# Splitting the attention logits, and a second feed-forward stage with six of its blocks by seven products

## The chip, the cores and the metric

The kernel runs on one core of one Trainium2 chip. The metric is the time of one execution on the device in microseconds (us). TensorE (PE in the profile) multiplies matrices; PEld is its loading of the stationary operand. VectorE (DVE), ScalarE (ACT) and GpSimd (POOL) do elementwise work. SyncE (SP) starts most of the transfers; GpSimd starts those that add into their target. Each engine works through a list of its own in order and waits on semaphores for the others.

## The reference, cut to what matters

One layer of a diffusion backbone: a half-step feed-forward layer, a mixer (attention beside an mLSTM), a second half-step feed-forward layer, a final norm. There are 256 latent tokens (x) and 256 context tokens (ctx), the width is 2048, the hidden width of a feed-forward layer 5632. All is in float32.

```python
def half_step_ffn(x, mod, i, g, w_up, w_down):
    h = adaln(x, g, mod, i)
    a, b = jnp.split(h @ w_up, 2, axis=-1)
    return x + 0.5 * mod[:, i + 2, None, :] * ((jax.nn.silu(a) * b) @ w_down)

def attend(q, k, v):
    s = jnp.einsum('bqhgd,bkhd->bhgqk', q, k, preferred_element_type=jnp.float32) * HEAD_DIM ** -0.5
    p = jax.nn.softmax(s, axis=-1).astype(v.dtype)
    return jnp.einsum('bhgqk,bkhd->bqhgd', p, v)
```

The second feed-forward layer and the attention have latent queries only (256 of them). There are 8 heads of 128, keys and values for 2 groups of 4 heads, and 512 keys. The modulation vectors mod[0] to mod[8] are products of a condition vector with nine 2048 by 2048 matrices; mod[8] is the gate of the second feed-forward layer's output.

## The kernel before, in words

**Split products.** A float32 product at full precision is made of three products of operands in the faster type fp32r: every operand x is split into hi (x rounded, by ACT) and lo (x minus hi, by DVE), and `mm3` (line 145) issues hi by hi, hi by lo and lo by hi. Weights are split as they arrive: `load_split` (line 138) has SP fetch 1 MB (128 by 2048) into one of 3 `raw` tiles, and `split` (line 117) turns it, in two halves of 1024 columns, into `hi` and `lo` tiles. There are four tiles of each, so four halves: ACT can start on a half when TensorE has released the half four before it. All rows of this splitting have the line numbers 125 (ACT) and 126 (DVE), all rows of the three products 147, 148 and 149.

**The order of the work.** The functions are Python generators that issue instructions unit by unit. A planner then orders each engine's list by program order and by when it reckons that operands are ready; an instruction marked `keep_in_program_order` stays where the program put it. Tiles of a pool with the same tag share a fixed number of slots, and a new tile waits for the slot's last reader.

**The attention.** `ev_kv` (line 1591) and `ev_q` (line 1603) norm and rotate keys and queries, turn them by TensorE transposes, and a DVE copy puts the turned tile into `kT` or `qT` in plain float32. `attention` (line 1648) then makes the logits of one head and 128 queries by 512 keys with one plain float32 product (line 1655), the softmax, its transposes and the product with the values `av`. There are 16 such logits. `kT` and `av` lie in the slot that the context half of `v1` (the mLSTM's values) has left; `qT` in the slot of `mqT`. While the queries are made, half of `hhi` and `hlo` (the normed input, 512 tokens) holds context columns that nobody reads any more.

**The second feed-forward stage.** The hidden width is cut into 11 blocks of 512 numbered 0 to 10. Block 0 is done ahead. Each other block's up projection is made in one of two ways:

- `up(n)` (line 2126): eight units, each of 1 MB of weights and 24 matmuls of 512 columns.
- `quad(n)` (line 2046): a Winograd form of the 2 by 2 product (tokens halves by width halves) that needs seven products instead of eight. Fourteen steps, each of 1 MB of weights and 12 matmuls. The sums of weights that it needs are made by transfers which add into the tile that they land in (`accum`, line 723, from GpSimd's queue): `chain_[q]` holds weights, is split, gets the next part added, is split again. The order of steps and what follows each is the table `order` at line 2103; X and Y are two banks of PSUM, each with one buffer, that the steps accumulate into and that ACT and DVE read out between steps.

`down(n)` (line 2160) is the down projection of a block: four units of 1 MB and 24 matmuls. It needs the block's hidden values in transposed form, which `turned` (line 2015) makes by transposes and a split into the two-slot tiles `hids`; a list `turn` keeps what waits for that. The loop at line 2204 issues unit after unit of `units` (ups and downs) and behind each the quad steps that are due by `PACE2` (line 39): step number below (u + 1) times 70/73. Quads are 1, 3, 5, 7, 9; ups are 2, 4, 6, 8, 10.

Beside this, `mod_late` (line 264) sums the 32 products of mod[8], one DVE instruction each, paced by calls of `load_split`; the pair (32, 62) says that product 32 is due at call 62, and two waits of 3 calls come on top. After the loop `before_final` (line 2191) drains what is left of them, writes the row of mod[8] to DRAM and has it spread from there over all partitions into `g8`, in the slot of `chain_[0]`. The down projection of block 9 and then that of block 10 (`last2`, line 2219) follow; they read `g8`, and in block 9 each finished piece gets the residual added by a transfer.

Of the kernel before, what the change touches and what calls it, by code (L numbers as in the profile page):

```python
# [19 lines left out]
P = 128  # L20
# [18 lines left out]
PACE2 = 70 / 73  # L39
# [17 lines left out]
def tile_layer(ctx: ExitStack, tc: tile.TileContext, I: dict, out: bass.AP):  # L57
# [1189 lines left out]
    with ExitStack() as mx:  # L1247
# [11 lines left out]
        v1 = {s: one([P, 2, NH, 130], f"v1{s}", tag="v1l" if s else "slotA") for s in (CTX, LAT)}  # L1259
        for s in (CTX, LAT):  # L1260
            nc.gpsimd.memset(v1[s][:, :, :, 128:130], 1.0)

        def ev_mv(h0, c0, bs):
            for t, b in bs.items():
                if c0:
                    nc.vector.tensor_tensor(gt[:, t, :], b[:, :32], gb, op=ALU.add)
                s, tt = divmod(t, 2)
                nh = (b.shape[1] - c0) // HD
                nc.scalar.activation(v1[s][:, tt, h0 : h0 + nh, 0:HD], b[:, c0:].rearrange("p (h d) -> p h d", d=HD), AF.Copy)
# [134 lines left out]
        def state(h, kTc):  # L1404
# [7 lines left out]
            for t in range(2):  # L1412
                for d in range(2):
                    nc.vector.tensor_scalar(vw[:, t, d, :], v1[CTX][:, t, h, :], wg[:, t, d, h : h + 1], None, op0=ALU.mult)
# [93 lines left out]
        def heads_out(h, t, E, A):  # L1508
            b = tbank()
            for d in range(2):  # L1510
                o = b[:, d * 130 : (d + 1) * 130]
                srcs = [(q, st_) for q, (st_, t_) in enumerate(PAIRS[d]) if t_ == t]
                for n, (q, st_) in enumerate(srcs):
                    nc.tensor.matmul(o, E[:, d, q, :], v1[LAT][:, st_, h, :], start=d == 0 and n == 0, stop=False, skip_group_check=True)
# [76 lines left out]
        def ev_kv(t, b):  # L1591
# [3 lines left out]
            def late():  # L1595
# [3 lines left out]
                nc.vector.tensor_copy(kT[:, :, t * P : (t + 1) * P], tb[:, :256].rearrange("p (g k) -> p g k", g=2))  # L1599
# [3 lines left out]
        def ev_q(c, t, b):  # L1603
            y = head_norm(b, 4, 0, t - 2)

            def late():
# [3 lines left out]
                nc.vector.tensor_copy(qT[:, 4 * c : 4 * c + 4, (t - 2) * P : (t - 1) * P], tb.rearrange("p (g k) -> p g k", g=4))  # L1610
# [8 lines left out]
        kvs = one([P, NKV * 512 + 4 * 256], "kvs", tag="slotA")  # L1619
        kT = kvs[:, : NKV * 512].rearrange("p (g k) -> p g k", g=NKV)  # L1620
        av = kvs[:, NKV * 512 :].rearrange("p (t c) -> p t c", t=4)
# [20 lines left out]
        qT = one([P, NH, T], "qT", tag="mqT")  # L1642
# [5 lines left out]
        def attention(kv):  # L1648
            items = [(t, g) for t in range(2) for g in range(4)]
            pr, pT, o = {}, {}, {}  # L1650
            for i in range(len(items) + 2):
                if i < len(items):
                    t, g = items[i]
                    b = bank()
                    nc.tensor.matmul(b, qT[:, 4 * kv + g, t * P : (t + 1) * P], kT[:, kv, :], start=True, stop=True)
# [243 lines left out]
    with f2x:  # L1899
# [53 lines left out]
        beside["load"] = mod_late(f8cm.__enter__(), 8, 9, ((32, 62),))  # L1953
# [3 lines left out]
        QUADS = range(1, LAST, 2)  # L1957
# [54 lines left out]
        turn = []  # L2012
        summed = set()

        def turned():
# [3 lines left out]
            n, t, sa, sign = turn[0]  # L2019
            if n >= 2 and n - 2 not in summed or n - 1 not in hids or (n - 1, 0) in [x[:2] for x in turn] or (n - 1, 1) in [x[:2] for x in turn]:  # L2020
                return
# [17 lines left out]
        def wait_turn(n, t, sa, sign):  # L2039
            turn.append((n, t, sa, sign))  # L2040
# [5 lines left out]
        def quad(n):  # L2046
# [40 lines left out]

            def again(q):
                if n + 2 in QUADS:
                    nc.sync.dma_start(chain_[q], part(n + 2, 0, q))  # L2090
# [6 lines left out]
            def plain(q):  # L2097
# [8 lines left out]
                (n1, held, "Y", True, chained(1, 2), kept),  # L2106
                (s4, loaded, "Y", False, lambda q: accum(ra[q], part(n, 1, q)), p35),
# [106 lines left out]
        while turn:  # L2214
            turned()
# [156 lines left out]
```

## Time and profile before

| what | value |
|---|---|
| median of 3 runs | 2615.98 us (2615.42 to 2619.67) |
| the profiled execution's own time | 2617.32 us |
| its span, first to last instruction | 2615.6 us |
| granted TensorE clock, mean | 0.996 |
| the attention's queries and logits | about 1700 to 1850 us |
| the second feed-forward stage | about 1940 us to the end |

The profile lists for each engine the busy time, for groups of instructions the count, mean duration and the idle time before them, and who ended that. Matmuls are pipelined: a row's duration (0.39 us for 512 columns) overlaps the next one's, so their price is read from the distance between starts. Rows of a timeline are: start, duration, engine, line, operation, result and operands, count.

### The profile page before, as it was taken

The page shows a single profiled execution, that of the slowest core. Times are in us where ns is not written, and L with a number is a line of the kernel's source. Part 1 is how long each engine was busy: PE and PEld are TensorE (multiplying, and loading weights), DVE is VectorE, ACT ScalarE, POOL GpSimd, SP SyncE. Part 2 cuts the span into 40 slices and gives each one's busy share as a digit, 9 for nine tenths or more (in the row PEclk, how much of TensorE's full clock was granted, in tenths as well). Part 3 has the DMA queues.
Part 4 walks back from the last instruction along what each step waited for, and adds up shares of the span by engine and source line. Part 5 has one row for each costly group of instructions (what it writes and reads, how often), then busy time and mean ns, then how long its engine had stood idle before and what let it go on. Part 6 is the DMA issues. An engine that isn't in the chain of part 4 may idle for free.

```text
span 2615.6 us, 33733 instructions
## 1 busy us (share of the span) xinstructions
PE 2593.2 (99%) x12727; PEld 2155.0 (82%) x12727; DVE 2117.8 (81%) x2856; ACT 1361.1 (52%) x1724; POOL 209.1 (8%) x263
## 2 busy tenths in 40 slices
PE   8999999999999999999999999999999999999998
PEld 5788888888888888888889889887898888888887
DVE  7788888878888788888887789788888777777867
ACT  5454444445444465444454437555576655555554
POOL 0000000100000100000110000120000000000001
PEclk8999999999999999999999999999999999999999
DMA  9989999999999998889986856665679998989975
GB/s 396 350 213 267 269 278 279 258 271 284 269 275 281 266 246 237 229 210 230 227 242 265 297 198 240 207 214 203 237 251 301 312 291 278 286 286 281 271 229 175
DMA packets 127219, 679.97 MB, mean 260 GB/s; under 512 B 14152, under 2 KB 16712, under 8 KB 65232
## 3 DMA queue, kind: packets, MB, share of 16 engines
q1 hardware_dynamic: 99696, 500.59, 51.6%
q0 software_dynamic: 27360, 177.22, 34.6%
q8 instruction: 100, 1.64, 0.2%
q14 instruction: 63, 0.52, 0.1%
HBM read 659.87 MB, written 17.89 MB: 259 GB/s over the span
## 4 chain that ended last, share of the span: by engine, by line
PE 88%; DVE 5%; DMA 4%; issue 2%; ACT 1%; POOL 0%; SPq 0%; POOLq 0%; ACTq 0%; DVEq 0%
PE mm L149 23%; PE mm L147 23%; PE mm L148 23%; DMA mraw<-in_w_m 2%; DVE lo L126 1%; PE mm L85 1%; PE tr L148 1%; PE Y L149 1%; PE Y L147 1%; PE Y L148 1%; PE tr L149 1%; PE tr L147 1%; PE X L147 1%; PE X L149 1%; PE X L148 1%
## 5 line engine op out<-in xcount | busy, mean ns | idle before, releaser
L125 ACT ACTIVATE hi<-raw 128x1024 fp32r<-128x1024 f32 (+3 forms) x536 | 556.6, 1042 | 601.4 <-PE mm L149 440.4
L126 DVE TENSOR_TENSOR lo<-raw,hi 128x1024 fp32r<-128x1024 f32 (+1 forms) x524 | 631.4, 1210 | 273.4 <-ACT hi L125 248.5
L125 ACT ACTIVATE hi<-chain 128x1024 fp32r<-128x1024 f32 x320 | 338.1, 1060 | 259.9 <-PE mm L149 141.1
L126 DVE TENSOR_TENSOR lo<-chain,hi 128x1024 fp32r<-128x1024 f32 x320 | 386.2, 1220 | 84.9 <-ACT hi L125 82.3
L147 PE MATMUL mm<-hi,hhi 128*128 128x512 f32 (+3 forms) x1024 | 394.1, 385 | 0.0
L149 PE MATMUL mm<-hi,hlo 128*128 128x512 f32 (+3 forms) x1024 | 387.0, 378 | 0.0
L148 PE MATMUL mm<-lo,hhi 128*128 128x512 f32 (+3 forms) x1024 | 386.8, 378 | 0.0
L205 DVE SCALAR_TENSOR_TENSOR junk<-sraw,cBh 128x1024 fp8e5<-128x1024 f32 x192 | 234.2, 1220 | 22.2 <-DMA sraw<-in_w_mt 19.9
L149 PEld LDWEIGHTS mm<-hi,hlo 128*128 128x128 f32 x1024 | 192.5, 188 | 33.8
L147 PEld LDWEIGHTS mm<-hi,hhi 128*128 128x128 f32 x1024 | 192.6, 188 | 31.2 <-issue 0.2
L148 PEld LDWEIGHTS mm<-lo,hhi 128*128 128x128 f32 x1024 | 192.8, 188 | 30.9 <-issue 0.2
L149 PE MATMUL mm<-hi,hid2l 128*128 128x512 f32 x352 | 137.4, 390 | 0.0
L147 PE MATMUL mm<-hi,hid2h 128*128 128x512 f32 x352 | 137.2, 390 | 0.0
L148 PE MATMUL mm<-lo,hid2h 128*128 128x512 f32 x352 | 137.1, 390 | 0.0
L148 PE MATMUL mm<-lo,h2hi 128*128 128x512 f32 x320 | 124.8, 390 | 0.6 <-DVE lo L126 0.6
L147 PE MATMUL mm<-hi,h2hi 128*128 128x512 f32 x320 | 124.8, 390 | 0.0
L149 PE MATMUL mm<-hi,h2lo 128*128 128x512 f32 x320 | 124.6, 390 | 0.0
L723 POOL DMA_DIRECT2D chain<-in_w_up1b x60 | 53.1, 885 | 723.3 <-DVE lo L126 645.5
L147 PE MATMUL mm<-hhi,hi 128*128 128x512 f32 (+1 forms) x288 | 101.1, 351 | 0.0
L149 PE MATMUL mm<-hhi,lo 128*128 128x512 f32 (+1 forms) x288 | 99.0, 344 | 0.0
L148 PE MATMUL mm<-hlo,hi 128*128 128x512 f32 (+1 forms) x288 | 98.8, 343 | 0.0
L205 DVE SCALAR_TENSOR_TENSOR sr<-sr,cBl 128x1024 f32<-128x1024 f32 x65 | 78.2, 1216 | 7.9 <-DMA gains<-in_k_gain 6.4
(499 smaller groups left out, 5458.6 us busy)
## 6 DMA issues: line engine op xcount, KB each, us to landing
raw<-in_w_dn SPq DMA_DIRECT2D x70, 1024.0 KB, 7.5
sraw<-in_w_mt SPq DMA_DIRECT2D x128, 512.0 KB, 7.9
chain<-in_w_up1b POOLq DMA_DIRECT2D x60, 1024.0 KB, 10.5
raw<-in_w_up2b SPq DMA_DIRECT2D x50, 1024.0 KB, 6.7
raw<-in_w_up1b SPq DMA_DIRECT2D x40, 1024.0 KB, 8.1
mraw<-in_w_m SPq DMA_DIRECT2D x32, 1024.0 KB, 7.6
sr<-in_w_mt SPq DMA_DIRECT2D x62, 512.0 KB, 5.5
chain<-in_w_dn POOLq DMA_DIRECT2D x30, 1024.0 KB, 9.9
```

The source lines that it names most:

```text
L85: ins = getattr(self.engine, name)(*a, **k)
L125: scalar[0].activation(hi, src, AF.Copy)
L126: vector[0].tensor_tensor(lo, src, hi.bitcast(F32), op=ALU.subtract)
L147: tensor[0].matmul(out_ap, sh, mh, start=first, stop=False, skip_group_check=skip)
L148: tensor[0].matmul(out_ap, sh, ml, start=False, stop=False, skip_group_check=skip)
L149: tensor[0].matmul(out_ap, sl, mh, start=False, stop=last, skip_group_check=skip)
L205: ins = nc.vector.scalar_tensor_tensor(junk() if junk else raw, raw, 1.0, cB[s], op0=ALU.mult, op1=ALU.mult, accum_out=mT[:, i, s, kt, h : ...
L723: accum = lambda dst, src: nc.gpsimd.dma_start(dst, src, accum_op=ALU.add)
```

## The change

Four things in one edit:

- **Logits.** The turned keys and queries are split into hi and lo (`high_low`: one ACT copy and one DVE subtraction) and the logits are made by `mm3`, three products in fp32r, in place of one in float32. The split keys and the first four heads' queries lie in the context columns of `hhi` and `hlo`; the other queries take the slot of `mqT`; the second group's keys are copied by ACT into `k1` before `hhi` is given back. `v1`'s context half becomes two tiles, whose slots `av` and `k1` take.
- **Blocks.** Quads are 1, 3, 5, 6, 8, 9; ups are 2, 4, 7, 10. So one block goes from `up` to `quad`. The order of units becomes up 2, down 0, up 4, down 1 to 3, up 7, down 4 to 6, up 10, down 7 and 8.
- **Pace.** Steps start six units later and are due by (u - 6) times 84/62 with units counted from 1: 84 steps in 62 units in place of 70 in 73. A step that needs a hidden tile turned waits for it (`ready`), and a hidden tile is turned one unit (after a quad) or two (after an up) later than it could be. The products of mod[8] are due later: product 1 at call 14, product 32 still at call 62.
- **A sum of weights.** In each quad, the transfer that added a part into `chain_[q]` after the step n1 goes. The same sum is made from the part that lies in `ra[q]` anyhow: for q = 0 by two GpSimd additions of 128 by 1024, for q = 1 by one DVE addition of 128 by 2048.

```diff
-PACE2 = 70 / 73
+PACE2 = 84 / 62
...
-                nc.vector.tensor_copy(kT[:, :, t * P : (t + 1) * P], tb[:, :256].rearrange("p (g k) -> p g k", g=2))
+                w = (slice(4 + t // 2, 8, 2), slice(t % 2 * P, (t % 2 + 1) * P))
+                high_low(hhi[:, *w], hlo[:, *w], tb[:, :256].rearrange("p (g k) -> p g k", g=2))
...
-                nc.vector.tensor_copy(qT[:, 4 * c : 4 * c + 4, (t - 2) * P : (t - 1) * P], tb.rearrange("p (g k) -> p g k", g=4))
+                w = slice((t - 2) * P, (t - 1) * P)
+                qh, ql = queries(c)
+                high_low(qh[:, :, w], ql[:, :, w], tb.rearrange("p (g k) -> p g k", g=4))
...
+        def high_low(hh, hl, x):
+            nc.scalar.activation(hh, x, AF.Copy)
+            nc.vector.tensor_tensor(hl, x, hh.bitcast(F32), op=ALU.subtract)
...
+        k1 = one([P, 2, 2, T], "k1", F32R, tag="slot1")
+        for x in range(2):
+            nc.scalar.activation(k1[:, x], keys[1][x].bitcast(F32), AF.Copy)
+        keys[1] = [k1[:, x] for x in range(2)]
...
-                    nc.tensor.matmul(b, qT[:, 4 * kv + g, t * P : (t + 1) * P], kT[:, kv, :], start=True, stop=True)
+                    qs = [x[:, g, t * P : (t + 1) * P] for x in queries(kv)]
+                    mm3(b.rearrange("p (a k) -> p a k", a=2), *qs, *keys[kv], True, True)
...
-        beside["load"] = mod_late(f8cm.__enter__(), 8, 9, ((32, 62),))
+        beside["load"] = mod_late(f8cm.__enter__(), 8, 9, ((1, 14), (32, 62)))
...
-        QUADS = range(1, LAST, 2)
+        QUADS = (1, 3, 5, 6, 8, 9)
...
-            turn.append((n, t, sa, sign))
+            turn.append((n, t, sa, sign, at_unit[0] + 1 + (sign > 0)))
...
+            def summed_weights(q):
+
+                if q:
+                    tc.keep_in_program_order(add(chain_[q], chain_[q], ra[q]))
+                else:
+                    for h in range(2):
+                        w = slice(h * 1024, (h + 1) * 1024)
+                        nc.gpsimd.tensor_tensor(chain_[q][:, w], chain_[q][:, w], ra[q][:, w], op=ALU.add)
+                accum(ra[q], part(n, 1, q))
...
-                (n1, held, "Y", True, chained(1, 2), kept),
-                (s4, loaded, "Y", False, lambda q: accum(ra[q], part(n, 1, q)), p35),
+                (n1, held, "Y", True, None, kept),
+                (s4, loaded, "Y", False, summed_weights, p35),
...
-            yield from up(2)
-            yield from down(0)
-            for n in (4, 6, 8):
+            for n, downs in ((2, (0,)), (4, (1, 2, 3)), (7, (4, 5, 6)), (10, (7, 8))):
                 yield from up(n)
-                yield from down(n - 3)
-                yield from down(n - 2)
-            yield from down(7)
-            yield from up(10)
-            yield from down(8)
+                for d in downs:
+                    yield from down(d)
...
+        def ready(i):
+
+            n, step = i // 14, i % 14
+            if step == 11:
+                return (QUADS[n], 0) in done
+            return not n or step not in (1, 7) or (QUADS[n - 1], step // 7) in done
...
-        for u, _ in enumerate(units()):
+        for u, _ in enumerate(units(), 1):
             steps(forms)
+            at_unit[0] = u
             turned()
-            while n_side < n_quads and n_side < (u + 1) * PACE2:
+            while n_side < n_quads and n_side < (u - 6) * PACE2 and ready(n_side):
                 next(side)
                 n_side += 1
                 turned()
```

More of the change, by code (lines that the diff above doesn't have):

```diff
@@ L1258, in tile_layer @@
         gt = one([P, 4, 32], "gt")
[L1259 removed]
+        v1l = one([P, 2, NH, 130], "v1l")
+        v1 = {CTX: [one([P, NH, 130], f"v1c{t}", tag=f"slot{t}") for t in range(2)], LAT: [v1l[:, t] for t in range(2)]}
         for s in (CTX, LAT):
[L1261 removed]
+            for t in range(2):
+                nc.gpsimd.memset(v1[s][t][:, :, 128:130], 1.0)
         def ev_mv(h0, c0, bs):
```

30 lines of the change are left out of this document (19 added, 11 removed).

## The prediction, made before the changed kernel ran

> **What bounds the kernel now.** I read the page first (shares, chain of waits), then what TensorE waited for, then windows over stages, then single instructions.
>
> ```profile
> span 2615.6 us, 33733 instructions
> PE 2593.2 (99%) x12727; PEld 2155.0 (82%) x12727; DVE 2117.8 (81%) x2856; ACT 1361.1 (52%) x1724; POOL 209.1 (8%) x263
> PE 88%; DVE 5%; DMA 4%; issue 2%; ACT 1%; POOL 0%; SPq 0%; POOLq 0%; ACTq 0%; DVEq 0%
> ...
> PE mm L148 <- DVE lo L126: 0.6, 1, 0.6
> ...
> ACT hi L125 <- PE mm L149: 183.7, 128, 3.0
> ...
> 100.00:1000.00 900.00, 898.08 (x4113) 738.57 (x4112) 745.07 (x922) 452.68 (x526) 77.78 (x88) 1.00 0.95 267
> 600.00:650.00 50.00, 50.00 (x230) 41.33 (x229) 45.09 (x62) 25.03 (x29) 2.64 (x3) 1.00 0.97 296
> 1940.00:2616.00 676.00, 665.65 (x3002) 550.75 (x3001) 521.25 (x566) 373.74 (x403) 43.03 (x50) 1.00 0.88 270
> 2050.00:2500.00 450.00, 450.00 (x2011) 372.11 (x2010) 344.28 (x368) 251.65 (x259) 27.02 (x31) 1.00 0.93 282
> ```
>
> TensorE is busy 99% and the chain is 88% TensorE. The line of PE's waits is the only one from 1950 us to the end: 0.6 us. The ACT line (same stage) says that the splitting of weights stands still because TensorE has not released its buffers: ACT and DVE run ahead and are held back, not the reverse. In the windows (columns: PE, PEld, DVE, ACT, POOL busy; clock; DMA share; GB/s) the second feed-forward stage has TensorE at 450.00 of 450 with DVE at 76.5% and the transfers at 93%. The first stage, built in the same way, has TensorE at 898.08 of 900 with DVE at 83%, and one 50 us stretch with DVE at 90% and no loss. So a matmul saved is time saved, and what is laid on DVE is free up to some 90%, as long as it doesn't come in lumps that eat the lead.
>
> **The change part by part.**
>
> ```profile
> 1953.08 0.39 PE L147 MATMUL X<-hi,h2hi 128*128 128x512 f32 x1
> ...
> 1955.80 0.39 PE L147 MATMUL mm<-hi,h2hi 128*128 128x512 f32 x1
> ...
> 1961.23 0.39 PE L147 MATMUL X<-hi,h2hi 128*128 128x512 f32 x1
> ...
> 1739.48 1.02 PE L1655 MATMUL mm<-kvs,qT 128*128 128x512 f32 x2
> 1740.34 0.60 PE L1669 MATMUL tr<-ident,pr 128*128 128x128 f32 x4
> ```
>
> *One block from up to quad.* From the first to the second row is one quad step, 12 matmuls: 2.72 us; to the third one up unit, 24 matmuls: 5.43 us. So 0.2265 us a matmul. An up is 8 units, 192 matmuls, 43.5 us; a quad 14 steps, 168 matmuls, 38.1 us. Saved: **5.4 us**. Both are followed by the same eight transposes. The stage goes from 76 units and 70 steps to 68 and 84.
>
> *Logits.* A float32 logit (two records) takes 1740.34 - 1739.48 = 0.86 us up to the next start; three fp32r matmuls of 512 columns take 3 x 0.2265 = 0.68 us. 16 x 0.18 = **2.9 us** saved. Bounds: 0 if the moving operand in two pieces of 256 costs its overhead again, 3.0 at most; I take 2.9, as plain matmuls of that size are the nearest row.
>
> ```profile
> L1610 DVE COPY qT<-tr 128x512 f32<-128x512 f32 x4 | 2.8, 692 | 0.6 <-PE tr L1609 0.5
> L1770 ACT ACTIVATE cathi<-cx 128x512 fp32r<-128x512 f32 x4 | 2.4, 624 | 0.3 <-DVE cx L1714 0.2
> 1700.00:1850.00 150.00, 150.00 (x758) 121.26 (x757) 122.34 (x209) 79.91 (x117) 18.61 (x20) 1.00 0.61 213
> ```
>
> *What feeds the logits.* The DVE copy (0.69 us for 512 columns) becomes an ACT copy (0.62 by the nearest row) and a DVE subtraction of about the old length: four of 512 and four of 256 columns, and two copies of 512 into `k1`. That is about 4 x 0.62 + 4 x 0.35 + 2 x 0.62 = 5 us more on ACT, in 150 us in which it works 80. Cost 0, covered by TensorE's projections; what can be late is the first logit of a group, by one 0.6 us operation, and it has other matmuls to change places with. Without that cover it would be two groups x 0.7 = 1.4 us.
>
> ```profile
> 2572.02 2.28 DVE L2231 TENSOR_TENSOR lo<-raw,hi 128x2048 fp32r<-128x2048 f32 x1
> ...
> q1 hardware_dynamic: 22076, 137.91, 54.0%
> q0 software_dynamic: 6912, 44.04, 33.6%
> chain<-in_w_up2b POOLq DMA_DIRECT2D x30, 1024.0 KB, 10.9
> chain<-in_w_up2b SPq DMA_DIRECT2D x10, 1024.0 KB, 6.3
> ra<-in_w_up2b POOLq DMA_DIRECT2D x10, 1024.0 KB, 11.4
> ```
>
> *Load of the other engines.* From 1 MB of weights DVE subtracts 2.28 us' worth. In the dense part (61 units, 84 steps: 61 x 5.43 + 84 x 2.72 = 560 us) there are 145 MB against 136 in 560 us before: +20 us; the DVE additions +6 x 2.28 = 14; the read-outs of more quads about +4. With 76.5% before that makes about 83%, the first stage's level. Transfers: adding ones go from 8 x 5 = 40 (the x30 and x10 from GpSimd's queue) to 6 x 6 = 36, plain ones of weights from 106 to 104. With MB and the share of 676 us in the q rows, at 0.336 x 676 / 44 = 5.2 us a MB for the adding and 0.54 x 676 / 138 = 2.6 for the plain that is 26 us of transfer time less in a stage 8 us shorter: 88% becomes 85%. No price. The next quad's first weights now have two steps to land (13 us, 17 before) against 6.3; four steps separate an adding transfer from its use (27 us) against 10.9 to 11.4. Both still fit.
>
> *Steps later and closer.* The products of mod[8] are packed into some 54 calls in place of 60, 0.1 us of DVE a unit. Steps run beside units 7 to 68, with their transfers on SP's and GpSimd's queues behind those units' loads. The first six units lose DVE work, so the 0.6 us wait goes (worth up to 0.6, not counted). Two steps now often follow each other without a unit between them. By the order table that matters where the second writes a bank that is still read out: a12 to n1 and n1 to s4, four places in all by the pace. Bounds 0 to 1.3 us each (one 0.7 us read-out and its wait); taken 0, because the next unit's matmuls are ready and in another bank.
>
> *The sum by GpSimd.* This is the only new wait.
>
> ```profile
> L1617 POOL TENSOR_TENSOR gm<-gm,mg x4: 1293/1516/1745, 1726.9 to 1757.5; 128x512 f32<-128x512 f32 x4
> ...
> 1728.80 2.31 DVE L126 TENSOR_TENSOR lo<-raw,hi 128x1024 fp32r<-128x1024 f32 x1
> ...
> 1756.05 3.18 POOL L1617 TENSOR_TENSOR gm<-gm,mg 128x512 f32<-128x512 f32 x2 [26.01 <-ACT gm L1616]
> ...
> 1757.99 2.32 DVE L126 TENSOR_TENSOR lo<-raw,hi 128x1024 fp32r<-128x1024 f32 x1
> ...
> L125 ACT ACTIVATE hi<-chain 128x1024 fp32r<-128x1024 f32 x320 | 338.1, 1060 | 259.9 <-PE mm L149 141.1
> L126 DVE TENSOR_TENSOR lo<-chain,hi 128x1024 fp32r<-128x1024 f32 x320 | 386.2, 1220 | 84.9 <-ACT hi L125 82.3
> ```
>
> GpSimd's one elementwise product of this kind takes 1.29 to 1.75 us for 512 columns, so an addition of 1024 about 2.6 to 3.5, two a quad 5 to 7 us. It starts when n1's split has read `chain_[0]`, four steps before s2 reads the sum, so the sum itself is never late, and the adding transfer queued behind it on GpSimd has four steps. But DVE: while GpSimd ran to 1759.23, a split issued at 1757.99 took 2.32 us in place of 1.22: it stood still until GpSimd ended (1759.23 + 1.1 = 1760.3). So per quad DVE may stand still for up to 5 us, in two lumps, and has the 2.28 us addition later. The lead that can hide it: three halves of 1.36 (step) or 2.72 us (unit), 4.1 to 8.2, less ACT's 1.06 and DVE's 1.22 for a split: 1.8 to 5.9 us. Bounds: 0 a quad, and 7.3 - 1.8 = 5.5 a quad (33 us). Nearest row: this one and its twin at 1728.80, where a held split cost TensorE nothing. I take 0.2 a quad, **1 us**. The Trainium skill ("SBUF — State Buffer", Who interferes with whom) says the same as the row, that a VectorE instruction with two SBUF inputs and a GpSimd one that reads SBUF lock each other out whole; the two rows agree with it. The Trainium skill ("GPSIMD Engine Reference", 3.1 Elementwise) has 4497 ns for an addition of 2048 columns on GpSimd, by which the two would be an estimated 4.5 us a quad, a little under the 5 to 7 of the rows.
>
> *The end.*
>
> ```profile
> 2497.64 1.22 DVE L205 SCALAR_TENSOR_TENSOR sraw<-sraw,cBl 128x1024 f32<-128x1024 f32 x1
> ...
> g<-mod SPq DMA_DIRECT2D x1, 1024.0 KB, 4.8
> mod<-gr SPq DMA_DIRECT2D x1, 8.0 KB, 3.1
> L1022 DVE SCALAR_TENSOR_TENSOR acc<-acc,g x8: 679/682/692, 2566.4 to 2587.0; 128x512 f32<-128x512 f32 x8
> ...
> 2540.48 0.68 DVE L2048 TENSOR_TENSOR ca<-Y,ca 128x512 f32<-128x512 f32 x1
> ...
> 2544.30 0.69 DVE L2032 SCALAR_TENSOR_TENSOR hid2l<-tr,hid2h 128x512 fp32r<-128x512 f32 x1 [0.81 <-ACT hid2h L2030]
> ```
>
> Before, the last step came four units ahead of the final downs; now it is the very last thing before them. Its read-out up to the split hidden tile takes 4.5 us (2540.48 to 2544.99), and only the token half t = 0 of block 9 can cover it: two pieces of 2.72 us, enough if the planner puts them there; 0 to 4.5. The last product of mod[8] falls on call 68, now the last unit: product, sums, transpose (about 3 us), store 3.1, load 4.8 make 11 us, and the first use is some 11 us later; late by 0 to 4, with four PSUM banks (10.9 us) behind it. Taken 0.
>
> Sum: -5.4 - 2.9 + 1 = -7.3. The profiled execution (span 2615.6, itself 2617.32) would come to 2610.0; it lies 1.3 above the median. From the median 2615.98: **2608.6 us**.
>
> **The rivals.**
>
> *GpSimd holds DVE back (slower).* Place: between n1 and s4 of each quad. For it: the 2.32 us row, and DVE at 83% plus 6 x 5 to 7 us of standing still, which is 89 to 91%. Against it: 90% was carried without loss in the first stage. It decides from (8.3 + 5.2) / 6 = 2.3 us of TensorE a quad, where the 8.3 saved are gone and 5.2 (0.2%) more; at 2.3 to 5.5 a quad the time is 2621 to 2641. Between 0.5 and 2.3 a quad it gives 2611 to 2621, no change that can be told. The rule of the Trainium skill on "SBUF — State Buffer" is this mechanism in general form.
>
> *The end is laid bare.* Read-out chain and `g8` together 4 to 8 us: 2613 to 2617, no change.
>
> *The logits do not get cheaper.* 2.9 us less gain: 2611.5. Nothing speaks for it but the two-piece operand.
>
> **How the numbers follow.** Forecast (all but 3 us of the 8.3 kept) 0.60; end bare 0.12; GpSimd middling 0.10, heavy 0.16; logits 0.02. About 0.2% (5.2 us) is what measurement can tell here: faster 0.60, same 0.24, slower 0.16. The range goes from 2605 (8.3, the 0.6 us wait, a little luck) to 2620, leaving the heavy case and a few hundredths out.
>
> **What would show it.** Right: 24 fewer up or quad matmuls and no L1655 float32 rows; steps still 2.72 us apart; PE's waits in the stage under 2 us; DVE about 83%. Wrong: lo rows of 2.3 us and more beside the GpSimd additions with PE waits on DVE lo; a gap in PE just ahead of block 9's down, ended by DVE or by the load of `g8`; PE waits on the read-outs of X or Y.

## The result and the profile after

The changed kernel takes 2625.62 us (median of 6, 2621.68 to 2630.77) against 2616.03 for the kernel before (median of 6, 2615.42 to 2619.67): the ratio is 1.0038, with an interval from 1.0028 to 1.0047. It is slower by 9.6 us where 7.3 us of gain were forecast. The profiled execution took 2623.24 us, 2.4 under its median.

From the page of the changed kernel, the span, the shares and the chain of waits, and the group of the second stage's lo by hi matmuls:

```profile
span 2621.5 us, 33785 instructions
PE 2590.5 (99%) x12719; PEld 2152.0 (82%) x12719; DVE 2164.4 (83%) x2878; ACT 1378.6 (53%) x1750; POOL 238.6 (9%) x273
...
PE 84%; DVE 7%; DMA 5%; issue 2%; ACT 1%; POOL 0%; ACTq 0%; POOLq 0%; DVEq 0%
...
L148 PE MATMUL mm<-lo,hid2h 128*128 128x512 f32 x352 | 138.3, 393 | 8.0 <-DVE lo L126 7.8
```

TensorE has less to do (12719 matmul records against 12727, 2590.5 us busy against 2593.2), and the span is longer all the same: the chain went from 88% TensorE to 84%, DVE's share from 5 to 7%. The chain only points the way: one per cent of the span is 26 us, and its shares move by more than the loss from one kernel to another (94% TensorE on the page of the kernel with the logits alone).

The timelines' rows of the second stage's first and last matmul of 512 columns, first of the kernel before, then of the changed one:

```profile
1947.61 0.40 PE L147 MATMUL mm<-hi,h2hi 128*128 128x512 f32 x1
...
2605.86 0.39 PE L149 MATMUL mm<-hi,hid2l 128*128 128x512 f32 x1
```

```profile
1943.66 0.40 PE L147 MATMUL mm<-hi,h2hi 128*128 128x512 f32 x1
...
2611.66 0.39 PE L149 MATMUL mm<-hi,hid2l 128*128 128x512 f32 x1
```

The stage took 668.0 us in place of 658.3. With a block as a quad it should have taken 658.3 - 5.4 = 652.8, so 15.2 us are lost in it. (What lies ahead of the stage varies by up to 7.6 us from one profiled execution to the next, so in what follows the stage is measured from its own first to its own last matmul, and whole kernels are compared by their medians.)

What TensorE waited for from 1930 us to the end, in the changed kernel (total, times, longest), and one window of it:

```profile
PE mm L148 <- DVE lo L126: 8.3, 9, 2.4
PE Y L148 <- DVE lo L126: 0.7, 1, 0.7
PE tr L2052 <- DVE ca L2074: 0.5, 1, 0.5
PE Y L147 <- ACT cy L2087: 0.4, 2, 0.2
PE mm L147 <- ACT hid2h L2055: 0.2, 1, 0.2
...
2000.00:2500.00 500.00, 491.15 (x2181) 401.99 (x2180) 410.98 (x407) 291.95 (x309) 58.87 (x42) 1.00 0.85 267
```

Before, there was one such wait of 0.6 us. Now TensorE waits nine times for a `lo` in mm. DVE is busy 82% of the window (410.98 of 500), close to the 83% that were forecast, but not for the reasons forecast: a split that stands still counts as busy, and 12 splits of the stage, all beside GpSimd's additions, took 19.7 us more in sum than the usual 1.22 us each. Without standing still DVE would be at some 78%, while the forecast had 83% without it and 89 to 91% with it. The transfers are at 85% in this window, but the same window of the kernel with the logits alone has 93%; over the whole stage (1940 us to the end) they are at 82%, where 85% was forecast and 88% stood before. So the engines had less to do than was reckoned, and the stage lost all the same.

One of the places, in the timeline of the changed kernel (TensorE, DVE, GpSimd):

```profile
2004.74 0.73 PE L147 MATMUL mm<-hi,hid2h 128*128 128x512 f32 x2
2007.92 0.51 PE L148 MATMUL mm<-lo,hid2h 128*128 128x512 f32 x1 [2.44 <-DVE lo L126]
...
2003.78 2.95 DVE L126 TENSOR_TENSOR lo<-chain,hi 128x1024 fp32r<-128x1024 f32 x1 [0.62 <-ACT hi L125]
2006.65 1.21 DVE L126 TENSOR_TENSOR lo<-raw,hi 128x1024 fp32r<-128x1024 f32 x1
2007.79 0.68 DVE L2073 TENSOR_TENSOR ca<-Y,ca 128x512 f32<-128x512 f32 x1
2008.39 2.82 DVE L126 TENSOR_TENSOR lo<-raw,hi 128x1024 fp32r<-128x1024 f32 x1
...
2003.24 2.40 POOL L2120 TENSOR_TENSOR chain<-chain,ra 128x1024 f32<-128x1024 f32 x1 [16.45 <-DVE lo L126]
2006.81 3.31 POOL L2120 TENSOR_TENSOR chain<-chain,ra 128x1024 f32<-128x1024 f32 x1 [1.16 <-DVE lo L126]
```

GpSimd adds from 2003.24 to 2005.64. The split that DVE issues at 2003.78 takes 2.95 us in place of 1.22: 1.86 us of waiting and 1.1 of work. Behind it in DVE's list stands the split of the unit's weights (2006.65), and that is the one TensorE waits for: from the starts 2004.74 and 2007.92, less two matmuls of 0.2265, 2.73 us. A gap is reckoned in this way throughout: from the start of one row to the start of the next, less 0.2265 us for each matmul of the row. Summed over all gaps of more than 0.25 us, TensorE lost 12.7 us in the stage (before: 0.76), 9.5 of them beside GpSimd's additions or just behind them: 2.7, 1.9, 0.6, 1.4, 2.5 and 0.4 in the six quads. The rest of the 15.2 is in smaller gaps.

### The profile page after: what moved, and what is told of

The parts are those of the page before. It is cut to its first block, busy times and chain, and to the rows that moved or that the text cites. A ratio compares the mean times of both kernels' runs of the same rounds, so it can differ in the third digit from the quotient of the medians.

```text
span 2621.5 us, 33785 instructions
## 1 busy us (share of the span) xinstructions
PE 2590.5 (99%) x12719; PEld 2152.0 (82%) x12719; DVE 2164.4 (83%) x2878; ACT 1378.6 (53%) x1750; POOL 238.6 (9%) x273
## 4 chain that ended last, share of the span: by engine, by line
PE 84%; DVE 7%; DMA 5%; issue 2%; ACT 1%; POOL 0%; ACTq 0%; POOLq 0%; DVEq 0%
PE mm L148 22%; PE mm L149 22%; PE mm L147 21%; DVE lo L126 3%; PE mm L85 2%; PE tr L149 2%; PE tr L148 2%; PE tr L147 2%; DMA raw<-in_w_dn 1%; DMA sraw<-in_w_mt 1%; PE Y L147 1%; PE Y L149 1%; PE Y L148 1%; PE X L147 1%; PE X L149 1%
## 5 line engine op out<-in xcount | busy, mean ns | idle before, releaser
L125 ACT ACTIVATE hi<-raw 128x1024 fp32r<-128x1024 f32 (+3 forms) x524 | 543.3, 1042 | 546.9 <-PE mm L149 380.0
L125 ACT ACTIVATE hi<-chain 128x1024 fp32r<-128x1024 f32 x336 | 354.7, 1059 | 288.2 <-PE mm L149 172.0
L126 DVE TENSOR_TENSOR lo<-chain,hi 128x1024 fp32r<-128x1024 f32 x336 | 413.8, 1245 | 100.7 <-ACT hi L125 99.0
L148 PE MATMUL mm<-lo,h2hi 128*128 128x512 f32 x256 | 100.0, 391 | 0.5 <-DVE lo L126 0.5
L149 PE MATMUL mm<-hi,h2lo 128*128 128x512 f32 x256 | 99.7, 389 | 0.0
L147 PE MATMUL mm<-hi,h2hi 128*128 128x512 f32 x256 | 99.1, 390 | 0.0
L148 PEld LDWEIGHTS mm<-lo,hid2h 128*128 128x128 f32 x352 | 66.1, 188 | 26.1 <-DVE lo L126 12.8
```

The lines of the kernel that those rows point to most:

```text
L125: scalar[0].activation(hi, src, AF.Copy)
L126: vector[0].tensor_tensor(lo, src, hi.bitcast(F32), op=ALU.subtract)
L147: tensor[0].matmul(out_ap, sh, mh, start=first, stop=False, skip_group_check=skip)
L148: tensor[0].matmul(out_ap, sh, ml, start=False, stop=False, skip_group_check=skip)
L149: tensor[0].matmul(out_ap, sl, mh, start=False, stop=last, skip_group_check=skip)
```

## The experiments

The theory after the result: GpSimd's additions, because they come in two lumps of 1024 columns, hold DVE back for longer than its lead at that place (the time by which a split is done before TensorE needs it). The rivals: the denser steps alone (84 in 62 units) eat the lead, by late transfers or by ACT's and DVE's own lists; the new order of turning; the logits. Times are medians; the kernel before stood at 2616.0 to 2616.7 beside them. The intervals are some 2.5 us to either side, so a difference of one or two us between two of these kernels is a hint and no more.

### The logits alone

The kernel before with the split logits and nothing else of the change (its diff is the part on logits shown above).

> The kernel before with the split logits alone. From the two traces (second stage's first matmul at 1943.7 in place of 1947.6 us): 2612 us, 3 to 4 us faster. If the gain were from another source than the logits, 2616 us.

Measured: 2613.42 us against 2616.30, ratio 0.9989 (0.9979 to 0.9999), so 2.9 us less. Its stage and one of its windows:

```profile
1942.88 0.40 PE L147 MATMUL mm<-hi,h2hi 128*128 128x512 f32 x1
...
2601.14 0.39 PE L149 MATMUL mm<-hi,hid2l 128*128 128x512 f32 x1
...
2000.00:2500.00 500.00, 500.00 (x2236) 413.43 (x2235) 380.76 (x406) 283.91 (x297) 30.44 (x35) 1.00 0.93 286
```

658.3 us for the stage, as before, and no gap in the window. So the logits bring what was forecast, as far as the interval can tell, and what went wrong lies in the second stage. With the block's 5.4 us on top, the changed kernel should have come to 2608.0. That is an estimate with the interval of this run, and the others are measured against it.

### The sums of weights, by one engine or another

Transfers again, everything else as changed:

```diff
-                (n1, held, "Y", True, None, kept),
-                (s4, loaded, "Y", False, summed_weights, p35),
+                (n1, held, "Y", True, chained(1, 2), kept),
+                (s4, loaded, "Y", False, lambda q: accum(ra[q], part(n, 1, q)), p35),
```

> The changed kernel with the sums of weights made by transfers again, as before the change; blocks, pace, delays and logits as changed. Theory A (GpSimd's additions hold VectorE's splits up, and TensorE with them): the waits beside the additions (9.5 us) go, and the DVE additions with them, 2610 to 2615 us. Theory B (the closer steps are too much for VectorE, with or without GpSimd): waits on the lo halves stay and the time stays above 2620 us. Theory C (the transfer was dropped because the transfers are the limit at this pace): slower than the changed kernel, waits on transfers.

Measured: 2616.18, ratio 1.0003 (0.9994 to 1.0013). It gives back 9.4 us of the 17.6 between 2625.6 and 2608.0, and 8.2 stay lost. Its stage and its waits:

```profile
1945.92 0.40 PE L147 MATMUL mm<-hi,h2hi 128*128 128x512 f32 x1
...
2605.84 0.39 PE L149 MATMUL mm<-hi,hid2l 128*128 128x512 f32 x1
...
PE mm L148 <- DVE lo L126: 2.3, 5, 0.7
PE tr L2052 <- DVE ca L2074: 1.5, 2, 1.2
PE Y L147 <- ACT cy L2087: 0.3, 2, 0.2
PE mm L147 <- ACT hid2h L2055: 0.3, 1, 0.3
```

659.9 us, 7.1 over 652.8; the waits for `lo` in mm fell from 8.3 to 2.3.

Both halves by DVE (this edit), then both by GpSimd (the two GpSimd additions stand for both q):

```diff
-                if q:
-                    tc.keep_in_program_order(add(chain_[q], chain_[q], ra[q]))
-                else:
-                    for h in range(2):
...
+                tc.keep_in_program_order(add(chain_[q], chain_[q], ra[q]))
```

> The changed kernel with both sums by VectorE (128 by 2048, 2.28 us each), none by GpSimd. A: no lumps of standing still, 2610 to 2615 us, although VectorE has 2.28 us a quad more to do of its own. B: more work for VectorE, so slower than the changed kernel, 2626 us and more.

> The changed kernel with both sums by GpSimd (four additions of 128 by 1024 a quad), none by VectorE. A: twice the dose, so some 9 us more, about 2635 us, with TensorE waits beside both additions. B: VectorE has 2.28 us a quad less to do, so faster than the changed kernel, 2620 us or less.

Measured: 2618.27 by DVE (1.0010, 1.0001 to 1.0019) and 2633.80 by GpSimd (1.0066, 1.0051 to 1.0081). Two DVE additions a quad cost 2.1 us more than the transfers, all six quads together; two halves by GpSimd cost 17.6 more, about twice the 9.4 of one half. So most of it is GpSimd's part, and it grows with the number of its additions.

GpSimd's half left out and nothing put in its place:

```diff
-                    for h in range(2):
-                        w = slice(h * 1024, (h + 1) * 1024)
-                        nc.gpsimd.tensor_tensor(chain_[q][:, w], chain_[q][:, w], ra[q][:, w], op=ALU.add)
+                    pass
```

> The changed kernel (2625.6 us) without GpSimd's two additions for q = 0; this half of that sum of weights is left out, DVE's addition for q = 1 stays. If GpSimd's additions cost by themselves what replacing them by transfers brought or more, this run is at 2613 to 2617. If the loss came from DVE's addition or from the other queues, it stays at 2621 to 2626.

Measured: 2613.91, ratio 0.9988 (0.9979 to 0.9998). GpSimd's twelve additions by themselves cost 2625.6 - 2613.9 = 11.7 us, 2.0 a quad. (This is by the medians alone.)

### Is it the amount of GpSimd's work, or the size of its pieces?

```diff
-                    for h in range(2):
-                        w = slice(h * 1024, (h + 1) * 1024)
+                    for h in range(8):
+                        w = slice(h * 256, (h + 1) * 256)
                         nc.gpsimd.tensor_tensor(chain_[q][:, w], chain_[q][:, w], ra[q][:, w], op=ALU.add)
```

> The changed kernel with GpSimd's half of the sum in eight additions of 128 by 256 in place of two of 128 by 1024. If the size of the lumps that VectorE stands still for is what makes TensorE wait: smaller lumps with VectorE's instructions between them, 2617 to 2621 us. If the total time of GpSimd's reading counts: 2625 us or more, since eight starts cost more than two.

Measured: 2617.35, ratio 1.0005 (0.9995 to 1.0014): 8.3 us less than in two lumps. The group of GpSimd's additions in the changed kernel:

```profile
L2120 POOL TENSOR_TENSOR chain<-chain,ra 128x1024 f32<-128x1024 f32 x12 | 33.4, 2787 | 107.3 <-DVE lo L126 107.3
```

The same group in eight pieces, with two DVE splits that run beside them:

```profile
L2120 POOL TENSOR_TENSOR chain<-chain,ra 128x256 f32<-128x256 f32 x48 | 66.6, 1421 | 103.9 <-DVE lo L126 103.9
...
2009.54 1.28 DVE L126 TENSOR_TENSOR lo<-chain,hi 128x1024 fp32r<-128x1024 f32 x1 [0.62 <-ACT hi L125]
2010.75 1.75 DVE L126 TENSOR_TENSOR lo<-raw,hi 128x1024 fp32r<-128x1024 f32 x1
```

GpSimd is busy for twice as long (66.6 us against 33.4), and the kernel is back within 1.2 us of the one with transfers (the stage takes 660.7 us, against 668.0 in two lumps and 659.9 by transfers). The longest split here takes 1.76 us, in the changed kernel 3.43: DVE gets its turn between two pieces. The sum of what the splits took over 1.22 us fell too, from 19.7 to 8.3 us. So the amount of GpSimd's work is not what counts, but how it holds DVE; whether by the longest hold or by the sum of them, this run alone doesn't tell. It also speaks against a rival, that the sum, or the adding transfer behind it, comes too late: in the first quad the eight pieces take 10.6 us from the first start to the last end (from 2009.00 us), the two lumps 6.9.

### What in GpSimd's work holds DVE

On the kernel with transfers, in each quad, GpSimd works on a dead tile that nobody else reads: four additions of 512 columns in one kernel, ten memsets of 512 columns in the other. Both are released by a tiny DVE copy.

```diff
+        scr = mT[:, 0:8].rearrange("p a b c d -> p (a b c d)")
+        nc.gpsimd.memset(scr, 0.0)
...
+            def beside_sum(q):
+                if not q:
+                    nc.vector.tensor_copy(scr[:, 0:1], chain_[q][:, 2047:2048])
+                    for _ in range(4):
+                        nc.gpsimd.tensor_tensor(scr, scr, scr, op=ALU.add)
+                chained(1, 2)(q)
...
-                (n1, held, "Y", True, chained(1, 2), kept),
+                (n1, held, "Y", True, beside_sum, kept),
```

> The kernel of the first experiment (sums by transfers) with four GpSimd additions of 128 by 512 of a dead tile to itself put in each quad where the changed kernel's additions run; nothing waits for them except the adding transfers behind them on GpSimd's queue. A (they lock VectorE out while they read): about as dear as the real additions, 2622 to 2626 us. Rival D (the dear part of the real additions is that the sum, or the adding transfer behind it, comes late): no dearer than without them, 2616 us.

> The same place with ten GpSimd memsets of 128 by 512 (0.53 us each by the trace of before, so 5.3 us, as long as the additions), which read nothing. A: 2616 us, as without them, because only reading collides with VectorE's second operand. If any GpSimd work in this place costs (its queue, its writing), 2622 us and more.

Measured: 2622.09 with additions (1.0026, 1.0015 to 1.0036), 2621.80 with memsets (1.0020, 1.0011 to 1.0029). The two times don't tell the theories apart, because the experiment had two faults. The tiny copy on DVE itself waited for an adding transfer, and DVE's splits stood behind it; and it ran, with GpSimd's work behind it, some 15 to 20 us ahead of the place of the real additions in each quad (in the kernel with additions at 1987.24 us in the first quad, where the changed kernel's begin at 2003.24). The waits of DVE in the kernel with memsets:

```profile
DVE mT L2132 <- DMA chain<-in_w_up2b: 12.2, 4, 5.3
```

What stands is the length of DVE's splits from `raw` in the two kernels, the one with additions first, then the one with memsets:

```profile
L126 DVE TENSOR_TENSOR lo<-raw,hi 128x1024 fp32r<-128x1024 f32 x167 | 217.0, 1315 | 64.7 <-ACT hi L125 64.0
```

```profile
L126 DVE TENSOR_TENSOR lo<-raw,hi 128x1024 fp32r<-128x1024 f32 x168 | 203.3, 1222 | 79.6 <-ACT hi L125 78.6
```

The mean is 1315 ns beside additions and 1222 beside memsets; it was 1219 to 1223 before and in the kernel with transfers, and 1292 in the changed kernel. Taken one by one, 23 splits of 1024 columns run while a memset does, and none takes longer than 1.23 us; 25 run while an addition does, and they take 1.85 us on average, up to 2.80. Additions stretch the splits, memsets don't. The Trainium skill ("SBUF — State Buffer", Who interferes with whom) has it that a VectorE instruction with two SBUF inputs contends with a GpSimd instruction that reads SBUF and not with one that only writes it; these two rows agree.

### The same sums at the old pace

The kernel before with the sums as in the change (with the function `summed_weights` of the change), in its five quads, 70 steps in 73 units:

```diff
-                (n1, held, "Y", True, chained(1, 2), kept),
-                (s4, loaded, "Y", False, lambda q: accum(ra[q], part(n, 1, q)), p35),
+                (n1, held, "Y", True, None, kept),
+                (s4, loaded, "Y", False, summed_weights, p35),
```

> The kernel before with one thing changed: the sum of weights after n1 made by two GpSimd additions of 1024 columns for q = 0 and one DVE addition for q = 1, in its five quads at the old pace. In six quads at the new pace this cost 9.4 us, 1.6 a quad. If a lump of GpSimd costs what it costs wherever it stands, five quads cost 5 x 1.6 = 8 us: 2624. If the denser steps (1.35 a unit in place of 0.96) are what leaves no lead to cover it, it costs less than 3 us here: 2616 to 2619.

Measured: 2618.40 against 2616.01, ratio 1.0005 (0.9995 to 1.0014; the ratio of the two medians is 1.0009). GpSimd's group and what TensorE waited for:

```profile
L2095 POOL TENSOR_TENSOR chain<-chain,ra 128x1024 f32<-128x1024 f32 x10 | 31.6, 3171 | 114.5 <-DVE lo L126 114.5
...
PE mm L148 <- DVE lo L126: 0.6, 1, 0.6
PE Y L148 <- DVE lo L126: 0.4, 1, 0.4
```

GpSimd's additions are even longer here (3171 ns), and they hold the splits just as long: 16.3 us over the usual in five quads, 3.3 a quad as in the changed kernel (19.7 in six), the longest split 3.43 us in both. Yet TensorE's waits are 1.0 us against the 9 of the changed kernel, and the cost is 1.3 us by the ratio and by the stage (659.5 against 658.3) and 2.4 by the medians: 0.3 to 0.5 a quad, which the interval can't tell from nothing, against 1.6 by the same comparison in the changed kernel. So the holding alone isn't what costs; it costs where the lead is too short to cover it. The likely reason for the shorter lead is the pace, 1.35 steps a unit in place of 0.96, but the two kernels also differ in the order of units, the start of the steps and the delay of turning, and no run has GpSimd's additions with the one and not with the others.

### Where the other 8 us go

Five quads in the order of units of the kernel before (ups 2, 4, 6, 8, 10); of the change, steps that start later (by four units), the delay of turning, `ready` and the later products of mod[8] are kept; sums by transfers:

```diff
-PACE2 = 84 / 62
+PACE2 = 70/68
...
-        QUADS = (1, 3, 5, 6, 8, 9)
+        QUADS = (1, 3, 5, 7, 9)
...
-            for n, downs in ((2, (0,)), (4, (1, 2, 3)), (7, (4, 5, 6)), (10, (7, 8))):
+            yield from up(2)
+            yield from down(0)
+            for n in (4, 6, 8):
                 yield from up(n)
...
-            while n_side < n_quads and n_side < (u - 6) * PACE2 and ready(n_side):
+            while n_side < n_quads and n_side < (u - 4) * PACE2 and ready(n_side):
```

> The changed kernel with the sums of weights by transfers, but with five quads and six ups as before (ups 2, 4, 6, 8, 10, the old order of units): steps four units later at 70 in 68, the delay of turning, the wait of a step for a turned tile and the later products of mod[8] stay. It does the matmuls of the split logits alone (2613.4 us). If the 8 us that are unaccounted for come from the sixth quad, that is from 84 steps in 62 units, it is at 2613 to 2615. If they come from the delay, the waits for turned tiles or the products of mod[8], it keeps most of them: 2619 to 2621.

Measured: 2615.26, ratio 0.9995 (0.9986 to 1.0005): 1.8 over the logits alone, which is within the spread. So the delay, `ready` and the products of mod[8] are not where the 8 us go. The kernel with the sixth quad, with 5.4 us less of matmuls, stands at 2616.18: the sixth quad gains nothing, and with what came along with it some 6 us are lost. That is the denser steps, the new order of units and a start two units later; these three were not tested one by one.

No delay of turning:

```diff
-            turn.append((n, t, sa, sign, at_unit[0] + 1 + (sign > 0)))
+            turn.append((n, t, sa, sign, 0))
```

> The changed kernel with the sums of weights by transfers (2616.2 us) and without the delay of turning: a hidden tile is turned as soon as it can be. By the change's parts that kernel should be at 2608 (logits alone 2613.4, less 5.4 for a block), so 8 us are unaccounted for. If the delay of turning costs them, because what waits for a turned tile (ready) holds back steps that then come in clusters, the time goes to 2608 to 2612. If the delay is what keeps the transposes from waiting for the read-out before them, it goes up: the 1.8 us of waits on DVE's ca grow, six quads and four ups with two tiles each of some 0.5 to 1 us, 2621 to 2630. If neither, it stays within 2 us of 2616.2.

Measured: 2621.62, ratio 1.0021 (1.0012 to 1.0030). Its waits:

```profile
PE tr L2052 <- DVE ca L2074: 4.8, 2, 2.8
PE mm L148 <- DVE lo L126: 2.3, 6, 0.7
```

The delay is worth 5.4 us: without it the transposes wait 4.8 us for the sum just before them, with it 1.5, which is 3.3 of the 5.4.

An earlier start of the steps: from the first unit, 84 in 67, with the products of mod[8] paced as before the change; and three units later, 84 in 65. The second edit:

```diff
-PACE2 = 84 / 62
+PACE2 = 84 / 65
...
-            while n_side < n_quads and n_side < (u - 6) * PACE2 and ready(n_side):
+            while n_side < n_quads and n_side < (u - 3) * PACE2 and ready(n_side):
```

> The kernel of the first experiment with steps from the first unit on, 84 in 67 units (1.25 a unit in place of 1.35), and the products of mod[8] paced as before the change. Theory B, for the rest of the loss (some 8 us that are left without GpSimd): the denser steps make it, so 2611 to 2613 us here. If the delay is needed (the forms of the tokens fill VectorE at the start of the stage): waits in the first 50 us of the stage and 2616 us or more.

> The changed kernel with the sums of weights by transfers (2616.2 us), steps three units later in place of six, due by 84 in 65: 1.29 a unit in place of 1.35. From the first unit on (84 in 67, 1.25 a unit) it was 2625.5, of which some 7 us were lost in the first 35 us of the stage, where ACT and DVE also make the forms of the tokens. If the pace is what costs, and the start is free again by the third unit, the time goes down by a third or so of the 8 us, to 2612 to 2615. If the start is the place of the loss, it goes up by 2 to 5: 2618 to 2621.

Measured: 2625.45 (1.0036, 1.0022 to 1.0049) and 2618.88 (1.0011, 1.0001 to 1.0020), that is 9.3 and 2.7 more than with six units' delay, though the pace is gentler. In the first 60 us of the stage, gaps of more than 0.25 us make 6 to 7 us in both, where the kernel with six units' delay has 0.9. The kernel that starts from the first unit loses as much again from 2160 to 2185 us, which was not followed up. The start is a place of loss of its own, and of the three that were tried six units is the best; a later one was not tried.

The adding transfers left out, first the twelve behind n1, then all 48 of the six quads:

```diff
-                (n1, held, "Y", True, chained(1, 2), kept),
+                (n1, held, "Y", True, None, kept),
```

```diff
-                return lambda q: accum(chain_[q], part(n, ab, c + q))
+                return lambda q: None
...
-                (s4, loaded, "Y", False, lambda q: accum(ra[q], part(n, 1, q)), p35),
+                (s4, loaded, "Y", False, None, p35),
```

> The kernel with all sums by transfers (e1_transfer, 2616.2 us) without the twelve adding transfers behind n1: the second split of the held weights takes them without that part, so this sum of weights is left out and nothing takes its place. It tells what those twelve transfers cost by themselves, which is the most that replacing them can bring. If late transfers are what the denser steps lose their 8 us to, taking 12 of the 48 adding ones away gives back 2 to 4: 2612 to 2614. If DVE's and ACT's own work in adjacent steps is, it stays within 1.5 of 2616.2.

> As the run before, but all 48 adding transfers of the quads are left out (the sums of weights are not made; every split, matmul and read-out stays). If the adding transfers, by slowing the plain loads that ACT then waits for, are what the denser steps lose, nearly all of the 8 us come back: 2608 to 2610. If the loss is in the lists of ACT and DVE (read-outs and splits of adjacent steps), the time stays at 2613 to 2617.

Measured: 2615.31 (0.9996, 0.9986 to 1.0005) and 2614.64 (0.9991, 0.9981 to 1.0000). Even with no adding transfer at all only 1.5 of the 8.2 us come back. So late transfers aren't the main cause, and the twelve that the change replaced cost 0.9 us, less than can be told from nothing: there was next to nothing to gain by replacing them. The stage without any adding transfer, its window and one of its places:

```profile
1942.97 0.40 PE L147 MATMUL mm<-hi,h2hi 128*128 128x512 f32 x1
...
2600.57 0.39 PE L149 MATMUL mm<-hi,hid2l 128*128 128x512 f32 x1
...
2000.00:2500.00 500.00, 498.35 (x2222) 410.30 (x2221) 392.44 (x412) 298.88 (x314) 0.00 (x0) 1.00 0.57 206
...
2001.29 0.39 PE L147 MATMUL Y<-hi,h2hi 128*128 128x512 f32 x1
...
2004.04 0.73 PE L147 MATMUL mm<-hi,hid2h 128*128 128x512 f32 x2
2005.49 0.50 PE L148 MATMUL mm<-lo,hid2h 128*128 128x512 f32 x1 [0.71 <-DVE lo L126]
...
2006.30 0.39 PE L147 MATMUL Y<-hi,n1f 128*128 128x512 f32 x1
...
2001.22 1.23 DVE L126 TENSOR_TENSOR lo<-chain,hi 128x1024 fp32r<-128x1024 f32 x1 [2.85 <-ACT hi L125]
2003.07 1.23 DVE L126 TENSOR_TENSOR lo<-chain,hi 128x1024 fp32r<-128x1024 f32 x1 [0.62 <-ACT hi L125]
2004.21 1.22 DVE L126 TENSOR_TENSOR lo<-raw,hi 128x1024 fp32r<-128x1024 f32 x1
```

The transfers are at 57%, and TensorE still stands for 1.65 us of the window. The stage takes 657.6 us, 4.8 over 652.8. The gaps of more than 0.25 us are: a12 to n1, 1.00 (at 2004) and 0.77 (at 2293); n1 to s4, 0.40 and 0.39; the start, 0.90; the end, 0.76. At a12 to n1 the step a12 (2001.29) and the step n1 (2006.30) are so close that DVE has n1's two `chain` halves to split before the unit's `raw` half, and only from 2001.22, when ACT got its buffers back; TensorE is through with what is split at about 2004.5 and waits until 2005.49. At this place it is work of ACT and DVE in their lists, and no transfer. At n1 to s4 TensorE waits for the read-out of the bank by ACT (`cy`, 0.3 us for the two places). The named gaps make 4.2 us, where the kernel before has 0.76; what is left of the 4.8 is in smaller gaps that were not followed up. Beside the stage's 4.8, 1.4 us are after the last matmul (11.2 us to the end, 9.8 in the kernel with the logits alone); why, no run shows.

## Why the prediction was wrong

- **One block from up to quad, -5.4:** the matmuls went as counted (24 fewer; the split logits add 16 records, so the page has 12719 for 12727). The time didn't follow: the sixth quad's gain is gone even without GpSimd (2616.2 us where 2608.0 was due).
- **Logits, -2.9:** right, as far as the interval can tell. Alone they bring 2.9 (2616.30 to 2613.42; the interval allows 0.3 to 5.5), and what feeds them cost nothing: TensorE has no wait between 1700 and 1850 us.
- **Load of the other engines, no price:** the load itself was reckoned too high (DVE at 78% without the splits' standing still, for 83%; transfers at 82% of the stage, for 85%), so that DVE shows 82% is luck. The conclusion, that such a load costs nothing, was wrong even so. The first stage's 90% without loss was taken as a limit for the second; the very sentence had the condition "as long as it doesn't come in lumps that eat the lead", and the sum went on without it.
- **Steps later and closer, taken 0:** the first step that failed. The four places, a12 to n1 and n1 to s4, are the right ones, and within the bounds of 0 to 1.3 us each: 1.00, 0.77, 0.40 and 0.39 us with no adding transfer. The mechanism that was named, a bank that is still read out, is only that of the two smaller ones, n1 to s4. At a12 to n1 it was another: the reason for taking 0, "the next unit's matmuls are ready", is what fell, since their weights stand behind the steps' in DVE's list. "The first six units lose DVE work, so the 0.6 us wait goes" was wrong too, 0.9 us are lost there. Not seen at all: the transposes that wait for DVE's `ca` (0.5 us in the changed kernel, 1.5 with transfers), small gaps, and a longer tail in some kernels. The whole term, with the load of the engines and the new order of units in it, measures 8.2 us by the medians; what the four places and the start leave of it was not followed to its places.
- **The sum by GpSimd, taken 1 us, bounds 0 to 33:** the step whose size failed most, 9.4 us against transfers and 11.7 by itself. The mechanism was the one described (splits of 2.82 and 2.95 us beside additions of 2.40 and 3.31). The price was taken from a place around 1758 us, where a held split cost nothing, as "the nearest row"; but that place is in another stage. In this stage, in the kernel before, the price was nearly right (0.3 to 0.5 us a quad, for 0.2); in the changed one it is 1.6 to 2.0. Of the 9.5 us of gaps beside the additions, 4.1 fall at the two places a12 to n1, where two steps come close; the other 5.4 fall elsewhere, so these places aren't the whole of it.
- **The end, 0:** nearly right. 0.41 and 0.48 us of waits in the changed kernel and the same 9.8 us behind the last matmul.
- **The rivals:** the heavy case, GpSimd holding DVE back, is the one that happened in kind. By its own measure, 2.3 us a quad, it wasn't heavy enough: at 1.6 to 2.0 a quad alone the kernel would have come to 2617 to 2620, no change that can be told. The other half came from the steps and what came along with them. Two costs were priced one by one, each near its lower bound, and they share one lead. That the pace had used it up when the additions came is the likely account; the run with the additions at the old pace fits it, without leaving the order of units and the delay of turning out.

The kernel that beats both is the one with the logits alone, 2613.4 us. Of the second stage's change no form that was run is below it: in small pieces it is at 2617.4, by transfers at 2616.2.

## What to carry to other kernels

A share of busy time says whether an engine can keep up on average, and it counts standing still as work. Whether a wait came up here depended on what could stand ahead of the next operand, against the lead at that place: the same 3.3 us of held splits a quad went with 9 us of TensorE's waits for DVE in one kernel and 1.0 in another. Before putting GpSimd beside a VectorE that reads two tiles from SBUF, look for the places where the lead is smallest, and cut GpSimd's work into pieces shorter than it: here the same sum cost 3.4 us in pieces of 256 columns and 11.7, more than all of the gain, in pieces of 1024. And when a change takes both some of the lead and something that is covered by it, price the two together.

## What the runs showed of the hardware that was not expected

- Twice as much GpSimd time (66.6 us in 48 pieces of 256 columns against 33.4 in 12 of 1024) cost 8.3 us less. A piece of 256 columns took 1.42 us on average, in which it also waits for DVE (the shortest took 0.73 us), so a quarter of the columns took half of the 2.79 us.
- GpSimd's memsets of 512 columns (539 ns each) leave the splits at 1222 ns, its additions of 512 columns stretch their mean to 1315, and that of the splits that run beside them to 1.85 us.
- A tiny DVE copy that waits for an adding transfer holds up all that stands behind it: in the kernel with memsets, which got 5.6 us slower, DVE stood for 5.3 us before one of them, and TensorE, waiting for the next split, for 3.4 us just behind.
- Kernels with the same work ahead of the second stage reach it between 1942.9 and 1950.5 us in their profiled executions: a difference of a few us between two single traces means nothing unless it is taken within the stage.
